# A hybrid decoder layer on one core: each head's first two token blocks projected side by side, and the norm's weights spread by TensorE

## The chip, the core and the metric

The kernel runs on one core of a Trainium2 chip. A core has five engines that run their own instruction streams in order: TensorE (PE in the profile, its weight loads PEld) multiplies matrices into PSUM, a memory of eight banks of 128 x 512 float32; VectorE (DVE), ScalarE (ACT) and GpSimd (POOL) work element by element; SyncE (SP) issues the DMA transfers here. They wait for each other by semaphores. The metric is the device time of one execution in microseconds.

## The reference

One layer of a decoder, in float32, over 1024 tokens of width 1024: an RMS norm, one wide input projection, two token mixers side by side, and a gated merge.

```python
h = rms_norm(x, norm_w)
proj = h @ w_in
q, k, v, z_a, xbc, z_s, dt_raw, gate_logits = split(proj)
# A: differential attention, 8 heads, two softmax maps per head
q, k = rms_norm(q, q_norm_w), rms_norm(k, k_norm_w)
a = softmax(q1 @ k1.T / 8) - lam * softmax(q2 @ k2.T / 8)      # causal
y_a = rms_norm(a @ v, subln_w) * 0.8 * silu(z_a)
# B: Mamba-2 scan, 32 heads in 4 groups, chunks of 128 tokens
x, B, C = split(silu(causal_conv(xbc)))
y_s = rms_norm((ssd_chunked(x, dt, A, B, C) + x * D) * silu(z_s), ssd_norm_w)
merged = sigmoid(g_a) * (y_a @ w_proj_attn) + sigmoid(g_s) * (y_s @ w_proj_ssd)
out = x + merged @ w_out
```

## The kernel before, in words

Every large product is made of three fast ones: each operand is split into a high part (rounded by ScalarE) and a low part (the rest, subtracted by VectorE or GpSimd), and TensorE adds high x high, high x low and low x high in one PSUM bank (`steps3`, L557; every matmul is recorded on L199, every transpose on L208).

A weight block is 128 rows by 512 columns. It is loaded raw from HBM (`w_loads`, four raw buffers for these), split into a slot (`w_splits`, L424; nine slots; every third block's low part is made on GpSimd, the others' on VectorE, L446), and its slot is given back by `w_done` (L546) when its last matmul has been issued. `w_need` (L540) waits for it.

The order of all instructions is written out by a planner (`Plan`, L79): generators for the bulk of TensorE's work and for all smaller tasks yield the time at which they can go on by the planner's own costs, and whichever is due emits its instructions next. On the chip each engine then keeps to that order. The bulk goes through these stages (`bulk`, L1757): the projections `pmz` of the first z groups and dt; twelve conv and gate pairs (`fX`, `fY`, `fZ`); eight heads (`att_proj`, L725) with attention and the scan worked in between as smaller tasks; then gates, output projections and the final product.

At the very start (`start`, L1778) SP issues the two halves of the first 128 tokens (x0), the norm's weights, four raw weight blocks and the other tokens. `prep_h` (L632) normalizes a block of 128 tokens: ScalarE squares and sums, GpSimd makes the root `rs`, VectorE multiplies x by `rs` and by the norm's weights (`stt`, L241, the tiles `nwb`), TensorE transposes the result (`ph`), and `h_evac` (L671) makes of it the high and low part, `hH` and `hL`, that all projections read. The norm's weights are 1024 numbers. Each half of them is loaded as 128 equal rows (L1781), 256 KB, and lies in SBUF until all eight blocks are prepared.

A head's projection (`att_proj`) takes for each of eight token blocks t the eight weight blocks kb in turn, three matmuls each, into one PSUM bank `pma`. In the first token block the weights are waited for, in the last one their slots are given back, one by one. After each token block `att_evac` (L748) is spawned: ScalarE squares q and k, takes z's tanh and copies v; VectorE sums the squares; GpSimd makes the root (`rs`, L265); VectorE scales q and k, after which the bank is free. PSUM banks are handed out by `trs`, eight in all, the bulk being served first. After four token blocks `qk_stack` transposes q and k and starts attention.

Of the kernel before, what the change touches and what calls it, by code (L numbers as in the profile page):

```python
# [139 lines left out]
def tile_hybrid_layer(ctx: ExitStack, tc: tile.TileContext, x, norm_w, w_in, q_norm_w, k_norm_w,  # L140
# [37 lines left out]
    def midt(shape=(P, 512), dt=F32, name="m"):  # L178
        return mid.tile(list(shape), dt, tag="b2", name=name)
# [31 lines left out]
    def pe_done():  # L211
        return pl.t + 0.2
# [40 lines left out]
    def load(o, i, after=0.0):  # L253
        nc.sync.dma_start(out=o, in_=i)
        q = pl.op("Q", 0.48, max(after, pl.t))
        n = o.free_size() * 512 / 360e3 if o.space != bass.MemoryType.DRAM else i.free_size() * 512 / 360e3
        return pl.op("D", n, q + 0.6) + lag[1]
# [282 lines left out]
    def w_need(i):  # L540
        while i not in w_at:
            yield pl.t + 0.1
        while w_at[i] > pl.t:
            yield w_at[i]
# [5 lines left out]
    def wide(i):  # L550
        return wts[i][:, 0].rearrange("p f c -> p (f c)"), wts[i][:, 1].rearrange("p f c -> p (f c)")
# [5 lines left out]
    def steps3(o, a, b, first, last, **kw):  # L557
        mm(o, a[0], b[0], first, False, **kw)
        yield
        mm(o, a[0], b[1], False, False, **kw)  # L560
        yield
        mm(o, a[1], b[0], False, last, **kw)
        yield
# [68 lines left out]
    def prep_h(t):  # L632
        while t not in xts:
            yield pl.t + 0.2
        xt, k, ats = xts[t]
        n = len(ats)
        parts = []
        for i, at in enumerate(ats):
            yield at
            ss = tin(1, "ss")  # L640
            xs = xt.rearrange("p (k c) -> p k c", k=KB)[:, i * KB // n:(i + 1) * KB // n]
            at = act(hL[:, i * KB // n:(i + 1) * KB // n, t * P:(t + 1) * P], xs, AF.Square, at,
                     scale=D ** -0.5, accum_out=ss)
            parts.append(ss)
        yield at
        rs = tin(1, "rs")
        if n > 1:
            at = stt(parts[0], parts[0], EPS, parts[1], ALU.add, ALU.add, at)
            yield at
            nc.gpsimd.tensor_tensor(out=rs, in0=parts[0], in1=mhalf[:, 0:1], op=ALU.pow)  # L650
            at = pl.op("G", 0.47, at)
        else:
            at = rsqrt(rs, parts[0], EPS, at)
        yield at
        pts = []
        nt = []
        for i in range(2):
            hs = slice(i * 512, i * 512 + 512)
            at = stt(xt[:, hs], xt[:, hs], rs, nwb[i], ALU.mult, ALU.mult, at - HOP if i else at)
            nt.append(at)  # L660
        for half in range(2):
            yield nt[half]
            kt = yield from pl.get(trs)
            pt = trt(f"ph{t}{half}")
            for i in range(4):
                tp(pt[:, i * P:(i + 1) * P], xt[:, (half * 4 + i) * P:(half * 4 + i + 1) * P])
            pts.append((pt, kt, pe_done()))
            pl.spawn(h_evac(t, half, *pts.pop()), pe_done())
        bigs.give(k, pl.t)
# [18 lines left out]
    def proj_tok(pm, t, ids, last):  # L688
        hb = lambda kb: (hH[:, kb, t * P:(t + 1) * P], hL[:, kb, t * P:(t + 1) * P])
        for kb in range(KB):  # L690
            yield from w_need(ids[kb])
            while (t, kb // 4) not in h_at:
                yield pl.t + 0.1
            while h_at[t, kb // 4] > pl.t:
                yield h_at[t, kb // 4]
            yield from steps3(pm, hb(kb), wide(ids[kb]), kb == 0, kb == KB - 1)
            if last:
                w_done(ids[kb])
# [26 lines left out]
    def att_proj(h):  # L725
        ids = w_next(KB)
        ks = []
        for _ in range(4):
            ks.append((yield from pl.get(heads)))
        v = bigt([P, NT, P], name=f"v{h}")  # L730
        zg = bigt([P, NT, P], name=f"zg{h}")
        kk = [bigt([P, S], F32R, name=f"kk{h}{m}") for m in range(2)]
        hd[h] = (v, zg, kk, ks)
        lefts[h] = [NT, {}]
        qk = []
        for t in range(NT):
            k = yield from pl.get(trs, first=True)
            pm = mmt(f"pma{h}{t}")
            yield from proj_tok(pm, t, ids, t == NT - 1)
            if t % 2 == 0:  # L740
                km = yield from pl.get(qkm)
                qk.append([midt([P, 2, 256], name=f"qk{h}{t}"), km, 0])
            pl.spawn(att_evac(h, t, pm, k, qk[-1][0][:, t % 2, :], qk[-1]), pe_done())
            if t % 4 == 3:
                pl.spawn(qk_stack(h, t // 4, qk), pl.t + 3.0)
                qk = []

    def att_evac(h, t, pm, k, qn, cell):  # L748
        v, zg = hd[h][0:2]
        at = pe_done()  # L750
        t2 = act(qn, pm[:, 0:256], AF.Square, at)
        t1 = act(zg[:, t, :], pm[:, 384:512], AF.Tanh, at, scale=0.5)
        tv = act(v[:, t, :], pm[:, 256:384], AF.Copy, at)
        yield t2
        ss = tin(4, "ss4")
        nc.vector.tensor_reduce(out=ss, in_=qn.rearrange("p (a d) -> p a d", a=4), axis=AX.X, op=ALU.add)
        t2 = pl.op("V", 0.335, t2)
        rs = tin(4, "rs4")
        yield max(t1, t2)
        t2 = rsqrt(rs, ss, 64 * EPS, t2)  # L760
        t1 = stt(zg[:, t, :], zg[:, t, :], 1.0, pm[:, 384:512], ALU.add, ALU.mult, t1)
        yield t2
        t2 = tt(qn.rearrange("p (a d) -> p a d", a=4), pm[:, 0:256].rearrange("p (a d) -> p a d", a=4),
                rs.unsqueeze(2).to_broadcast([P, 4, 64]), ALU.mult, t2)
        trs.give(k, max(t2, tv))
        cell.append(t2)

    def qk_stack(h, half, qk):
        v, zg, kk, _ = hd[h]
        lo, hi = slice(0, 64), slice(64, P)  # L770
        cs = slice(half * 512, half * 512 + 512)
        while len(qk[0]) < 5 or len(qk[1]) < 5 or "consts" not in ready:
            yield pl.t + 0.2
        yield max(qk[0][3:] + qk[1][3:] + [ready["consts"]])
        kq = yield from pl.get(bigs)
        kz = yield from pl.get(qlos)
        qh, ql = bigt([P, 2, 512], F32R, name=f"qh{h}{half}"), qlo[kz]
        done = []
        for isk in range(2):
            k = yield from pl.get(trs)  # L780
            pt = trt(f"pq{h}{half}{isk}")
            for i in range(4):
                tp(pt[:, i * P:(i + 1) * P], qk[i // 2][0][:, i % 2, isk * P:(isk + 1) * P])
            if isk:
                for c in qk:
                    qkm.give(c[1], pl.t + 0.1)
            at = pe_done()
            yield at
            t1 = at
            for m, (own, other) in enumerate(((lo, hi), (hi, lo))):  # L790
                if isk:
                    t1 = act(kk[m][own, cs], pt[own], AF.Copy, at)
                else:
                    act(qh[own, m], pt[own], AF.Copy, at, scale=wqk_c[own])
                    t1 = act(qh[other, m], pt[own], AF.Copy, at, scale=wqk_c[own])
            yield t1
            for m, (own, other) in enumerate(((lo, hi), (hi, lo))):
                if isk:
                    t1 = tt(kk[m][other, cs], pt[own], kk[m][own, cs], ALU.subtract, t1 - HOP)
                else:  # L800
                    t1 = stt(ql[own, m], pt[own], wqk_c[own], qh[own, m], ALU.mult, ALU.subtract, t1 - HOP)
            done.append(t1)
            trs.give(k, t1)
        pl.spawn(att_core(h, half, (qh, ql, kq, kz)), max(done))
# [967 lines left out]
            yield from products(c)  # L1772
        yield from final()

    kn = [mids.take() for _ in range(2)]
    nwb = [midt(name=f"nwb{i}") for i in range(2)]

    def start():  # L1778
        load_x(0)
        for i in range(2):  # L1780
            load(nwb[i], norm_w[:, i * 512:i * 512 + 512].partition_broadcast(P).rearrange("p a d -> p (a d)"))  # L1781
        yield from w_loads(0, 4)
        load_x(1)
        pl.spawn(prep_h(0))
        pl.spawn(prep_h(1), pl.t + 0.01)
        pl.spawn(w_splits(), pl.t + 0.02)
        yield from w_loads(4, 8)
        for t in range(2, NT):
            load_x(t)
            pl.spawn(prep_h(t))  # L1790
        while len(h_at) < 2 * NT:
            yield pl.t + 1.0
        for k in kn:
            mids.give(k, pl.t)

    def rest():
        yield pl.t + 8.0
# [34 lines left out]
```

## Time and profile before

| | us |
|---|---|
| median of 3 runs | 1624.73 (1622.62 to 1625.15) |
| the profiled execution | 1625.04 |
| its span, first to last instruction | 1623.3 |
| TensorE busy | 1589.2 (98%) |
| VectorE busy | 1088.5 (67%) |
| ScalarE busy | 915.1 (56%) |
| GpSimd busy | 706.9 (44%) |
| granted TensorE clock, mean | 0.996 of full |

A matmul's row lasts longer than its share of TensorE, since the next one starts before it ends: at full clock rows of 512 columns last about 0.39 us and start 0.23 us apart. Idle time in the views is time in which no row is open.

### The profile page before, as it was taken

To read this page: it belongs to the slowest core of one execution; us is meant where nothing else is said; L and a number is where in the kernel's file an instruction comes from. 1 tells how busy PE (TensorE), PEld (TensorE's weight loads), DVE (VectorE), ACT (ScalarE), POOL (GpSimd) and SP (SyncE) were. 2 spreads that over 40 slices of the span, in tenths; PEclk is the share of its full clock that TensorE was granted. 3 is DMA by queue.
4 is the path that set the end of the run, shared out by engine and by line. 5 is a ranking of instruction groups with operands and counts; after the bars stand their busy time and mean duration, and the time that the engine had idled before them with its cause. 6 is when DMAs were issued, how large, how long until landed. Compare 5 with 4: busy or idle time off the path is not lost.

```text
span 1623.3 us, 24344 instructions
## 1 busy us (share of the span) xinstructions
PE 1589.2 (98%) x8010; PEld 1330.2 (82%) x8010; DVE 1088.5 (67%) x2011; ACT 915.1 (56%) x2215; POOL 706.9 (44%) x847
## 2 busy tenths in 40 slices
PE   7999999999999999999989999999999999999999
PEld 5788888888788888887878888887887888888887
DVE  7836567537782576876767777876556577798831
ACT  7534447445563475786766777776666565352220
POOL 4315445334542543546475746464756433323000
PEclk9999999999999999999999999999999999999999
DMA  6213343533453461425163432433426397698941
GB/s 210 92 55 105 112 145 111 168 101 114 125 168 107 121 183 61 131 79 182 40 207 128 145 90 85 120 101 103 155 80 206 99 310 253 207 340 254 317 153 65
DMA packets 223804, 236.47 MB, mean 146 GB/s; under 512 B 15285, under 2 KB 155326, under 8 KB 223678
## 3 DMA queue, kind: packets, MB, share of 16 engines
q1 hardware_dynamic: 223678, 234.93, 45.6%
q8 instruction: 63, 1.03, 0.3%
q14 instruction: 63, 0.52, 0.1%
HBM read 164.48 MB, written 70.39 MB: 145 GB/s over the span
## 4 chain that ended last, share of the span: by engine, by line
PE 73%; DVE 3%; ACT 2%; POOL 2%; DMA 2%; issue 1%; SPq 0%; POOLq 0%; DVEq 0%; ACTq 0%
PE pma L199 18%; PE py L199 6%; PE pmz L199 5%; PE po L199 5%; PE pO L199 4%; PE pz L199 4%; PE px L199 4%; PE sc L199 4%; PE av L199 4%; PE fYc L199 3%; PE fXc L199 2%; PE pg L199 2%; PE pa L208 2%; PE fZc L199 2%; PE fYg L199 1%; PE pS L199 1%
## 5 line engine op out<-in xcount | busy, mean ns | idle before, releaser
L199 PE MATMUL pma<-w,hH 128*128 128x512 f32 x1024 | 345.2, 405 | 6.0 <-POOL w L233 5.4
L199 PEld LDWEIGHTS pma<-w,hH 128*128 128x128 f32 x1024 | 188.6, 189 | 40.9 <-POOL w L233 6.6
L199 PE MATMUL pma<-w,hL 128*128 128x512 f32 x512 | 206.8, 404 | 0.0
L199 PE MATMUL pmz<-w,hH 128*128 128x512 f32 x512 | 164.1, 398 | 0.7 <-ACT hH L225 0.7
L233 POOL TENSOR_TENSOR rawf<-rawf,rawf 128x512 f32<-128x512 f32 x54 | 71.6, 1326 | 166.4 <-DVE wp L233 87.8
L225 ACT ACTIVATE p<-p,nm 128x256 f32<-128x256 f32 (+7 forms) x128 | 98.6, 773 | 33.6 <-DVE nm L831 32.9
L225 ACT ACTIVATE w<-raw 128x512 fp32r<-128x512 f32 (+1 forms) x122 | 75.1, 626 | 75.0 <-DMA raw<-in_w_in_dram 28.7
L199 PEld LDWEIGHTS pmz<-w,hH 128*128 128x128 f32 x512 | 96.5, 190 | 20.6 <-ACT hH L225 1.1
L199 PEld LDWEIGHTS pma<-w,hL 128*128 128x128 f32 x512 | 96.8, 189 | 16.4
L233 POOL TENSOR_TENSOR w<-raw,w 128x512 fp32r<-128x512 f32 (+1 forms) x38 | 51.3, 1351 | 134.5 <-ACT w L225 120.7
L199 PE MATMUL fYc<-ft,wp 128*128 128x512 f32 x432 | 106.5, 392 | 0.7 <-DVE fu L233 0.7
L199 PE MATMUL pmz<-w,hL 128*128 128x512 f32 x256 | 101.4, 396 | 0.0
L199 PEld LDWEIGHTS fYc<-ft,wp 128*128 128x128 f32 x432 | 81.1, 189 | 17.9 <-DVE fu L233 1.1
L225 ACT ACTIVATE wp<-rawp 128x512 fp32r<-128x512 f32 x72 | 44.2, 626 | 84.1 <-POOL rawp L233 23.9
L233 DVE TENSOR_TENSOR wp<-rawf,wp 128x512 fp32r<-128x512 f32 x72 | 59.1, 837 | 34.7 <-ACT wp L225 34.7
L233 DVE TENSOR_TENSOR w<-raw,w 128x512 fp32r<-128x512 f32 (+1 forms) x84 | 65.1, 782 | 23.5 <-ACT w L225 23.3
L225 ACT ACTIVATE ab<-ab,nac 128x128 f32<-128x128 f32 x256 | 78.4, 392 | 1.7 <-POOL ab L1234 1.5
L199 PEld LDWEIGHTS av<-v,at 128*128 128x128 f32 x576 | 72.8, 191 | 6.5 <-ACT at L225 2.6
L265 POOL TENSOR_TENSOR rs<-rs,mhalf 128x4 f32<-128x4 f32 (+1 forms) x71 | 75.4, 1062 | 5.9
L225 ACT ACTIVATE wp<-rawf 128x512 fp32r<-128x512 f32 x108 | 65.9, 626 | 20.0 <-POOL rawf L233 16.4
L199 PE MATMUL av<-v,at 128*128 128x128 f32 x576 | 75.1, 275 | 1.7 <-ACT at L225 1.7
L831 DVE CUSTOM_DVE_ANT_0 p<-sc,maskb 128x512 f32<-128x512 f32 (+3 forms) x128 | 72.1, 584 | 6.2 <-PE sc L199 3.9
(299 smaller groups left out, 4217.8 us busy)
## 6 DMA issues: line engine op xcount, KB each, us to landing
raw<-in_w_in_dram SPq DMA_DIRECT2D x104, 256.0 KB, 3.6
rawf<-in_w_in_dram SPq DMA_DIRECT2D x72, 256.0 KB, 3.7
ab<-act_d SPq DMA_DIRECT2D x32, 512.0 KB, 4.9
cv_d<-cv SPq DMA_DIRECT2D x48, 256.0 KB, 2.1
t_d<-ts SPq DMA_DIRECT2D x24, 512.0 KB, 3.1
z_d<-zs SPq DMA_DIRECT2D x32, 256.0 KB, 2.0
xr<-cv_d SPq DMA_DIRECT2D x32, 256.0 KB, 3.0
zc<-z_d SPq DMA_DIRECT2D x32, 256.0 KB, 3.0
```

Source lines behind the costliest of these rows:

```text
L199: nc.tensor.matmul(o, lhsT=lhsT, rhs=rhs, start=start, stop=stop, **kw)
L208: nc.tensor.transpose(out=o, in_=i, identity=ident if idn is None else idn)
L225: nc.scalar.activation(o, i, f, **kw)
L233: (nc.vector if eng == "V" else nc.gpsimd).tensor_tensor(out=o, in0=a, in1=b, op=op)
L265: nc.gpsimd.tensor_tensor(out=dst, in0=dst, in1=mhalf[:, 0:cols], op=ALU.pow)
L831: nc.vector.tensor_tensor_reduce(out=p[:, j:e], in0=sc[i][:, 0:e - j], in1=maskb[:, S - n + j:S - n + e], scale=-1.0, scalar=nms[i - 1] if ...
```

## The change

Two things are changed. The heads' projections take the first two token blocks together: for each weight block kb first the three matmuls of block 0, then the three of block 1, into two PSUM banks. Blocks 2 to 7 go on as before. And the norm's weights are loaded as two rows of 512 numbers; a float32 matmul with a row of 128 ones spreads each to 128 rows of a PSUM bank, which VectorE then reads. The two banks are taken out of the eight until all token blocks are prepared. The two SBUF buffers that held the spread weights hold the rows now.

```diff
@@ prep_h
         pts = []
         nt = []
+        while "nwb" not in ready:
+            yield pl.t + 0.1
+        at = max(at, ready["nwb"])
+        yield at
         for i in range(2):
@@ att_proj
-        for t in range(NT):
-            k = yield from pl.get(trs, first=True)
-            pm = mmt(f"pma{h}{t}")
-            yield from proj_tok(pm, t, ids, t == NT - 1)
-            if t % 2 == 0:
-                km = yield from pl.get(qkm)
-                qk.append([midt([P, 2, 256], name=f"qk{h}{t}"), km, 0])
-            pl.spawn(att_evac(h, t, pm, k, qk[-1][0][:, t % 2, :], qk[-1]), pe_done())
-            if t % 4 == 3:
-                pl.spawn(qk_stack(h, t // 4, qk), pl.t + 3.0)
+        for ts in ((0, 1), (2,), (3,), (4,), (5,), (6,), (7,)):
+            pms = []
+            for t in ts:
+                k = yield from pl.get(trs, first=True)
+                pms.append((mmt(f"pma{h}{t}"), k))
+                if t % 2 == 0:
+                    km = yield from pl.get(qkm)
+                    qk.append([midt([P, 2, 256], name=f"qk{h}{t}"), km, 0])
+            for kb in range(KB):
+                yield from w_need(ids[kb])
+                for t, (pm, k) in zip(ts, pms):
+                    yield from steps3(pm, hblk(kb, t), wide(ids[kb]), kb == 0, kb == KB - 1)
+                    if kb == KB - 1:
+                        pl.spawn(att_evac(h, t, pm, k, qk[-1][0][:, t % 2, :], qk[-1]), pe_done())
+                if ts[0] == NT - 1:
+                    w_done(ids[kb])
+            if ts[-1] % 4 == 3:
+                pl.spawn(qk_stack(h, ts[0] // 4, qk), pl.t + 3.0)
                 qk = []
@@ before start
-    kn = [mids.take() for _ in range(2)]
-    nwb = [midt(name=f"nwb{i}") for i in range(2)]
+    kn, kb_ = [mids.take() for _ in range(2)], [trs.take() for _ in range(2)]
+    nwr = [midt([1, 512], name=f"nwr{i}") for i in range(2)]
+    nwb = [trt(f"nwb{i}") for i in range(2)]
+    one = const.tile([1, P], F32, name="one")
+    nc.gpsimd.memset(one, 1.0)
+
+    def norm_rows(t):
+        yield t
+        for i in range(2):
+            mm(nwb[i], one, nwr[i], True, True)
+        ready["nwb"] = pe_done()
@@ start
-            load(nwb[i], norm_w[:, i * 512:i * 512 + 512].partition_broadcast(P).rearrange("p a d -> p (a d)"))
+            t = load(nwr[i], norm_w[:, i * 512:i * 512 + 512])
+        pl.spawn(norm_rows(t), t)
```

Since the planner decides the order, its places move. On TensorE, the fourth head's first token block before: `pma30` and `pma31` are its first two token blocks, w76 to w83 its eight weight blocks, the other names attention and scan work of earlier heads.

```order
L199 MATMUL pma30_8248<-w76_7257,hH_111 128x512 x2
L199 MATMUL pma30_8248<-w76_7257,hL_112 128x512
L208 MATMUL pa230_8256<-ident_96,p23_8017 128x128 x4
L199 MATMUL pma30_8248<-w77_8141,hH_111 128x512 x2
L199 MATMUL pma30_8248<-w77_8141,hL_112 128x512
L199 MATMUL pma30_8248<-w78_8189,hH_111 128x512 x2
L199 MATMUL pma30_8248<-w78_8189,hL_112 128x512
L199 MATMUL av23_8275<-v2_7160,at230_8261 128x128 x4
```

Between the first matmul on w76 and the first on w78 stand six projection matmuls and one group of transposes. Now the same place on TensorE, from w77 on:

```order
L199 MATMUL pma30_8234<-w77_8096,hH_111 128x512
L199 MATMUL pma30_8234<-w77_8096,hL_112 128x512
L199 MATMUL pma31_8251<-w77_8096,hH_111 128x512 x2
L199 MATMUL pma31_8251<-w77_8096,hL_112 128x512
L199 MATMUL pma30_8234<-w78_8137,hH_111 128x512 x2
L199 MATMUL pma30_8234<-w78_8137,hL_112 128x512
L199 MATMUL pma31_8251<-w78_8137,hH_111 128x512 x2
L199 MATMUL pma31_8251<-w78_8137,hL_112 128x512
L199 MATMUL pma30_8234<-w79_8162,hH_111 128x512 x2
```

Each weight block is now followed by six matmuls instead of three before the next one is needed. On VectorE at the start before, the scalings of the last two token blocks (`x6`, `x7`) among the low parts `hL` of earlier ones, a block for dt (`w8`) and a small reduction:

```order
L233 TENSOR_TENSOR hL_112<-ph30_313,hH_111 128x4x128
L233 TENSOR_TENSOR hL_112<-ph31_321,hH_111 128x4x128
L241 SCALAR_TENSOR_TENSOR x6_200<-x6_200,rs_369,nwb0_118 128x512
L241 SCALAR_TENSOR_TENSOR x6_200<-x6_200,rs_369,nwb1_119 128x512
L233 TENSOR_TENSOR w8_349<-raw8_233,w8_349 128x4x32
L233 TENSOR_TENSOR hL_112<-ph40_353,hH_111 128x4x128
L233 TENSOR_TENSOR lp_273<-lamt_274 128x128
L312 TENSOR_REDUCE ls_408<-lp_273 128x2
L233 TENSOR_TENSOR hL_112<-ph41_362,hH_111 128x4x128
L241 SCALAR_TENSOR_TENSOR x7_202<-x7_202,rs_393,nwb0_118 128x512
```

and now the same place on VectorE:

```order
L233 TENSOR_TENSOR hL_112<-ph30_325,hH_111 128x4x128
L241 SCALAR_TENSOR_TENSOR x6_203<-x6_203,rs_374,nwb0_120 128x512
L241 SCALAR_TENSOR_TENSOR x6_203<-x6_203,rs_374,nwb1_121 128x512
L233 TENSOR_TENSOR hL_112<-ph31_334,hH_111 128x4x128
L233 TENSOR_TENSOR w8_357<-raw8_237,w8_357 128x4x32
L233 TENSOR_TENSOR hL_112<-ph40_361,hH_111 128x4x128
L241 SCALAR_TENSOR_TENSOR x7_205<-x7_205,rs_395,nwb0_120 128x512
```

The two pairs have moved ahead of one and of three other instructions, and the tiles `nwb0` and `nwb1` are PSUM banks. On ScalarE at the start, the splits `w0` to `w3` and the first copies `hH`, now (before, the split of `w2` stood behind the first copy):

```order
L225 ACTIVATE w0_151<-raw0_131 128x512
L225 ACTIVATE w1_156<-raw1_133 128x512
L225 ACTIVATE w2_164<-raw2_135 128x512
L225 ACTIVATE hH_111<-ph00_158 128x4x128
L225 ACTIVATE w3_173<-raw3_137 128x512
```

One split has moved ahead of the first copy. From the end of this start to the first head, and from the last head's end on, TensorE's order is that of before.

## Rows read from the trace of the kernel before

**Rows 1.** Busy time by stage (start, us, then each engine's busy time, clock, DMA).

```profile
0.00:40.00 40.00, 29.48 (x140) 22.61 (x141) 28.99 (x43) 30.72 (x58) 18.52 (x31) 1.00 0.65 213
40.00:598.00 558.00, 553.45 (x2548) 456.96 (x2547) 348.89 (x568) 287.06 (x549) 230.49 (x195) 0.99 0.39 119
598.00:1243.00 645.00, 631.37 (x3610) 538.94 (x3609) 453.04 (x1019) 448.44 (x1333) 357.86 (x542) 1.00 0.38 117
```

**Rows 2.** TensorE's waits, 598 to 1243 us (us, times, longest).

```profile
PE pma L199 <- POOL w L233: 5.4, 3, 2.3
PE pc L199 <- ACT yt L225: 2.3, 1, 2.3
...
PE pma L199 <- ACT w L225: 0.5, 1, 0.5
```

**Rows 3.** Timeline of TensorE, fourth head (start, us, what, count, idle before).

```profile
832.33 0.50 PE L199 MATMUL pma<-w,hH 128*128 128x512 f32 x1 [0.92 <-POOL w L233]
...
839.78 0.50 PE L199 MATMUL pma<-w,hH 128*128 128x512 f32 x1 [2.16 <-POOL w L233]
```

**Rows 4.** Busy time and granted clock of three stretches.

```profile
752.00:760.00 8.00, 5.70 (x30) 4.51 (x29) 3.58 (x5) 7.85 (x18) 5.74 (x5) 1.00 0.74 238
419.30:426.10 6.80, 6.80 (x24) 6.10 (x25) 4.31 (x9) 1.69 (x4) 0.00 (x0) 0.50 0.88 223
845.90:849.30 3.40, 3.02 (x9) 2.39 (x10) 3.23 (x5) 3.34 (x7) 2.49 (x3) 0.50 0.98 334
```

**Rows 5.** Timeline of TensorE, start.

```profile
7.56 2.33 PE L208 MATMUL ph<-ident,x 128*128 128x128 f32 x8 [7.56 <-DVE x L241]
10.64 1.22 PE L199 MATMUL pmz<-w,hH 128*128 128x512 f32 x2 [0.75 <-ACT hH L225]
...
15.50 0.63 PE L199 MATMUL pmz<-w,hL 128*128 128x512 f32 x1
...
17.54 0.40 PE L199 MATMUL pmz<-w,hL 128*128 128x512 f32 x1
17.77 0.40 PE L199 MATMUL pmz<-w,hH 128*128 128x512 f32 x1
```

**Rows 6.** Timeline of VectorE, start.

```profile
6.76 0.75 DVE L241 SCALAR_TENSOR_TENSOR x<-x,rs,nwb 128x512 f32<-128x512 f32 x1 [1.54 <-DMA nwb<-in_norm_w_dram]
7.97 0.75 DVE L241 SCALAR_TENSOR_TENSOR x<-x,rs,nwb 128x512 f32<-128x512 f32 x1 [0.46 <-DMA nwb<-in_norm_w_dram]
9.20 0.69 DVE L233 TENSOR_TENSOR w<-raw,w 128x512 fp32r<-128x512 f32 x1 [0.47 <-ACT w L225]
```

**Rows 7.** One tile's rows, `pacum`, float32 (ns min/median/max, first and last start).

```profile
L199 PE MATMUL pacum<-tv,tri x2: 377/378/378, 95.8 to 96.0; 128*128 128x256 f32 x2
```

**Rows 8.** DMA issues, 0 to 12 us (count, KB, us to landing), and SP's timeline.

```profile
x<-in_x_dram SPq DMA_DIRECT2D x2, 256.0 KB, 2.9
...
1.69 0.90 SPq L254 DMA_DIRECT2D nwb<-in_norm_w_dram  x2
```

**Rows 9.** GpSimd's rows on the tile `rs`, 598 to 1243 us.

```profile
L265 POOL TENSOR_TENSOR rs<-rs,mhalf x63: 1033/1045/1984, 604.7 to 1239.8; 128x4 f32<-128x4 f32 x63
```

**Rows 10.** VectorE's scalings, of the tiles `nwb` and `fXc`.

```profile
L241 DVE SCALAR_TENSOR_TENSOR x<-x,rs,nwb x16: 739/748/1783, 6.8 to 35.7; 128x512 f32<-128x512 f32 x16
...
L241 DVE SCALAR_TENSOR_TENSOR cv<-fXc,cols,cv x36: 733/742/751, 129.8 to 577.0; 128x511 f32<-128x511 f32 x12, 128x510 f32<-128x510 f32 x12, 128x509 f32<-128x509 f32 x12
```

**Rows 11.** Timelines of VectorE, GpSimd and TensorE, 29 to 38 us.

```profile
29.36 2.44 DVE L241 SCALAR_TENSOR_TENSOR x<-x,rs,nwb 128x512 f32<-128x512 f32 x2
...
34.74 2.76 DVE L241 SCALAR_TENSOR_TENSOR x<-x,rs,nwb 128x512 f32<-128x512 f32 x2
...
33.98 5.91 POOL L233 TENSOR_TENSOR r<-hH,hL 128x512 f32<-128x512 f32 x4 [1.03 <-DVE lp L233]
...
35.91 0.63 PE L208 MATMUL ph<-ident,x 128*128 128x128 f32 x4 [0.78 <-issue]
...
37.64 0.63 PE L208 MATMUL ph<-ident,x 128*128 128x128 f32 x4 [0.87 <-DVE x L241]
```

More of the change, by code (lines that the diff above doesn't have):

```diff
@@ L735, in att_proj, with hblk @@
         qk = []
-        for t in range(NT):
-            k = yield from pl.get(trs, first=True)
-            pm = mmt(f"pma{h}{t}")
-            yield from proj_tok(pm, t, ids, t == NT - 1)
-            if t % 2 == 0:
-                km = yield from pl.get(qkm)
-                qk.append([midt([P, 2, 256], name=f"qk{h}{t}"), km, 0])
-            pl.spawn(att_evac(h, t, pm, k, qk[-1][0][:, t % 2, :], qk[-1]), pe_done())
-            if t % 4 == 3:
-                pl.spawn(qk_stack(h, t // 4, qk), pl.t + 3.0)
+        for ts in ((0, 1), (2,), (3,), (4,), (5,), (6,), (7,)):
[16 more added lines that the diff above has]
+                pl.spawn(qk_stack(h, ts[0] // 4, qk), pl.t + 3.0)
                 qk = []
+    def hblk(kb, t):
+        return hH[:, kb, t * P:(t + 1) * P], hL[:, kb, t * P:(t + 1) * P]
     def att_evac(h, t, pm, k, qn, cell):
@@ L1792, in start @@
             yield pl.t + 1.0
-        for k in kn:
+        for k, b in zip(kn, kb_):
             mids.give(k, pl.t)
+            trs.give(b, pl.t)
     def rest():
```

## The prediction

> **What bounds the kernel now.** I read the busy time by stage first. The reader is to see that TensorE is the bound nearly everywhere: 553.5 of 558.0 us in the front-pair stage, 631.4 of 645.0 in the heads' stage, and 29.5 of 40.0 at the start [rows 1]; the last stage, 380 us behind the heads, looks like the second. So time can only come out of TensorE's idle time (34 us in all), and out of stretches in which its clock is at half. Two of the four stages are touched. The order of TensorE's instructions in the changed kernel is that of before from the end of the start to the first head, and again behind the last head, so I let those 558 and 380 us stand as they are, whatever they hold.
>
> Then I read who waited for whom in the heads' stage. Of its 13.6 us of idle time, 5.4 us are three waits of a head's matmul for a block of weights whose low part GpSimd makes, and 0.5 us one wait for a high part from ScalarE; the rest is spread over attention and state work, with one wait of 2.3 us for a scan chunk's product as its largest piece [rows 2]. The timeline of the fourth head's start shows two of them: the second matmul on block 2 (of 0 to 7) stands 0.92 us, that on block 5 2.16 us [rows 3]. All lie in a head's first token block. There eight blocks are taken in one pass, each for three matmuls, while their slots have only just come free in the last token block of the head before. From the second token block on all eight lie ready.
>
> [...]
>
> Last the start. TensorE's first row begins at 7.56 us, its first projection at 10.64 us, and its rows take 0.63 us each until 15.5 us and 0.40 from 17.5 us on: half clock first, full clock later [rows 5]. VectorE's first two scalings wait for the broadcast norm weights and end at 8.72 us, and the first subtraction of a weight block comes only at 9.20 us, since the weights queue behind those 512 KB [rows 6].
>
> **The change part by part.** First the heads. What it adds there is nothing: the same 1536 matmuls, in another order. The second token block's three matmuls on a block of weights are put behind the first's, so block n is first needed 3n matmuls later. Matmuls on these shapes start 0.23 us apart at full clock (17.54 and 17.77 [rows 5]), so three take 0.69 us. The wait on block 2 is moved by 1.4 us, against 0.92; that on block 5 by 3.4 us, against 2.16; the third, 2.3 us in the head before, is on block 7 and moved by 4.8 us. Each move exceeds its wait by half or more. What makes the blocks, the splits on ScalarE, VectorE and GpSimd, is paced by slots that come free in the head before, which is unchanged. So I take 5.4 us of the 5.9 as gone; the bounds are 5.9 (all) and 0 (the supply slips by as much).
>
> What is late next in this stage: both first blocks end three matmuls apart and are evacuated together. GpSimd's root takes 1.05 us for each [rows 9], and the second block's PSUM bank is held that much longer, while one bank more is held during the pass. With eight heads the bounds are 0 and 8 x 1.05 = 8.4 us if TensorE waited each time. Between them I take 0.7: in the trace other work of attention stands in a head's first blocks, and it fills such a gap as long as it has banks. For the rest of the stage, whose order is shuffled, I assume the old 7.7 us of other idle time; it could move by 3 us either way.
>
> The clock: 3.4 us at half cost 1.7 us [rows 4]. Two of the waits before it go, the scan product's 2.3 us may stay. I take half, 0.8 us, between 1.7 and 0; a new drop elsewhere, of 3.4 us or 6.8, would cost 1.7 to 3.4.
>
> Now the start. Removed: two transfers of 256 KB. Added: two of 2 KB, a memset, and two float32 matmuls of one row by 512 columns. A float32 product of 256 columns is two rows that start 0.2 us apart, so 0.4 us at full clock [rows 7]. At 512 columns that is 0.85, and at half clock 1.7 us each. A 256 KB transfer lands 2.9 us after its issue; by that the two rows, issued when the old ones were (two from 1.69 on, the second 0.45 later [rows 8]), are there by 4.6 and 5.05, the products at 6.3 and 8.0, and the two scalings end at 7.1 and 8.8, against 7.51 and 8.72. So the first transposes move hardly at all. If the small rows land 1 us later, so does all this; if earlier, up to 1 us is won. What does move is behind it: with the weights' raw blocks landing earlier, the first subtraction can follow the scalings at once, 8.8 instead of 9.20, and ScalarE, which now has three splits ahead of its first copy instead of two, finds them landed. Four weight blocks and x2 wait in SP's queue for these subtractions, so they are issued earlier by 0.4 and growing to about 1 us.
>
> VectorE's scalings are the other half. Alone one takes 0.74 to 0.75 us, but the slowest took 1.78 [rows 10]: the pairs at 29.36 and 34.74 took 2.44 and 2.76 us instead of 1.4 while GpSimd added hH and hL, and TensorE stood 0.78 and 0.87 us for transposes [rows 11]. 36 of the convolution's scalings, which read PSUM, never took over 0.751, with GpSimd at work in their stage too. So with the norm weights in PSUM I let the 2.4 us of excess go from VectorE (bounds 0 and 2.4).
>
> A scaling that reads PSUM took a median of 742 ns and one that reads SBUF alone 748 [rows 10], so I charge nothing for the other memory. [...]
>
> TensorE's idle time after its first projection is what these can give back: 10.5 us in the first 40 [rows 1], less 7.56 before its first row and 0.75 before the first projection, is 2.2, of which the two above are 1.65. I take 1.5, bounds 0 and 2.2. TensorE now begins 3 us earlier, so its clock may rise sooner; from 10.64 us to 16.5, the middle of the two rows that show half and full [rows 5], it lost half of 5.9, 2.9 us. I take a fifth, 0.6, bounds 0 and 2.9. The first projection itself waits for ScalarE's copy, which has the splits out of its way: 0.4, bounds -1 (small rows late) and 1. So the start gives 2.5 us, bounds -1 and 6.1. Two PSUM banks of eight are held until the last token block is prepared; the order of TensorE in the start shows the transposes no later than before relative to the projections, so I put nothing on it.
>
> **Sum**, against the profiled execution's own 1625.0 us (span 1623.3 and 1.7 around it): 5.4 + 0.8 + 2.5 - 0.7 = 8.0 us less, 1617.0. The median of the runs, 1624.7, lies 0.3 below that execution, which is inside the spread of the three.
>
> **Rivals.** (1) The waits come back in another place of the heads' stage: TensorE gets to the third token block as early as it saved, and stands there for attention's chains, whose speed the change does not touch. For it: 7.7 us of the stage's idle time are such waits. Against it: TensorE was busy 98% of the stage, so most chains are ahead of it. Then only the start pays: 1625.0 - 2.5 = 1622.5.
> (2) Slower: the double evacuation. The 8 PSUM banks run short behind each head's first pair, since the second block's bank waits for GpSimd's second root. It decides from the point where TensorE stands over 1 us per head, (5.4 + 2.5 + 0.8)/8 = 1.1. At 1.7 us per head, with other work of GpSimd's in between, it is 8 x 1.7 - 8.7 = 5 us slower: 1630. For it: GpSimd's roots already held VectorE in that stage. Against: the two roots together take 2.1 us, and the third token block's 24 matmuls that follow last at least 24 x 0.23 = 5.5.
> (3) The float32 products come late and the start gives nothing, while the heads pay: 1625.0 - 5.5 = 1619.5.
> (4) All pays: 5.9 of the waits, the drop's 1.7, and 4.5 at the start with an earlier full clock: 1613.
>
> **How the numbers follow.** Forecast 1617.0: chance 0.45, its own range 1614 to 1620. Rival 1: 0.20; rival 2: 0.13; rival 3: 0.10; rival 4: 0.12. A difference of 0.2% (3.2 us) is about what can be told from none here. Faster by more than that: forecast, rivals 3 and 4, and a quarter of rival 1, 0.72. Within: the rest of rival 1, 0.15. Slower: 0.13. The range leaves out the outer half of rival 4 and most of rival 2: 1610 to 1626.
>
> **What would show it.** Right: no wait of a head's matmul for w on GpSimd over 0.5 us in the heads' stage; TensorE idle there 8 to 9 us instead of 13.6; no 0.50 stretch near 846 us, the one near 419 still there, some 2 us earlier; scalings all at 0.75 us; no stand of TensorE at 34 to 38 us; the first head's first matmul 2 to 3 us before 597.8. Wrong: new waits for pma or its evacuation behind each head's first pair; or waits for sc, pa, av that have grown by as much as w lost; the first transposes later than 8.5 us.

## The result and the profile after

The changed kernel took 1614.34 us (median of 4 runs, 1612.54 to 1615.75), the kernel before 1623.67 beside it (4 runs, 1620.62 to 1625.15). The ratio is 0.9944 with a 95% interval of 0.9926 to 0.9963: faster by 0.56%, 9 us. Timed again later, the changed kernel took 1614.28 us and the ratio was 0.9946 (0.9933 to 0.9958). Forecast were 1617.0 us and a range of 1610 to 1626.

Of the changed kernel, busy time by stage, cut at its own first and last matmul of the heads (`pma`): start and end in us, length, busy time of PE, PEld, DVE, ACT, POOL with instructions, granted clock, DMA share, GB/s. The last row is the heads' stage of before, cut in the same way.

```profile
0.00:40.00 40.00, 34.65 (x158) 25.41 (x159) 27.68 (x50) 33.03 (x60) 15.78 (x32) 1.00 0.60 200
40.00:591.70 551.70, 547.17 (x2534) 451.35 (x2533) 346.22 (x561) 284.81 (x546) 232.75 (x195) 1.00 0.40 120
591.70:1227.70 636.00, 626.07 (x3597) 535.05 (x3596) 454.20 (x1016) 445.52 (x1330) 356.05 (x539) 1.00 0.38 118
```

```profile
597.80:1239.30 641.50, 627.87 (x3595) 536.35 (x3594) 452.21 (x1015) 447.22 (x1329) 354.50 (x536) 1.00 0.38 116
```

TensorE's idle time in the heads' stage fell from 641.50 - 627.87 = 13.6 us to 9.9, and the stage from 641.5 to 636.0. What it waits for there now, of the changed kernel (us in total, times, longest):

```profile
PE py L208 <- ACT xn L225: 2.8, 3, 1.3
PE av L199 <- ACT at L225: 1.5, 1, 1.5
PE pb L208 <- ACT yt L225: 1.3, 1, 1.3
PE pya L208 <- ACT at L225: 1.2, 1, 1.2
PE pa L208 <- DVE p L241: 1.0, 2, 0.6
```

The waits of `pma` for w, first in [rows 2], are gone without a rest. So is the wait of `pc`, second there with 2.3 us. In their place stand waits of attention and of the scan for ScalarE. They are of two kinds. `py` and `av` wait for an operand (`xn`, `at`) that ScalarE makes. `pb` and `pya`, as `pc` before, read nothing that the named instructions write: as the program has it, they wait for a bank of PSUM that ScalarE copies out (`yt` out of an earlier `pya`, `at` out of an earlier `pa`). One wait for an operand falls into the fourth head's first pair, where [rows 3] had the waits for blocks 2 and 5 (timeline of TensorE; the bracket is the idle time before and what ended it):

```profile
823.63 0.40 PE L199 MATMUL pma<-w,hH 128*128 128x512 f32 x1
825.37 0.66 PE L208 MATMUL py<-ident,xn 128*128 128x128 f32 x4 [1.34 <-ACT xn L225]
```

The clock near [rows 4], of the changed kernel: neither stretch is at half in this execution. In a second profiled execution of the same kernel the one behind 416 us is there again. First the changed kernel's first profiled execution, then its second:

```profile
419.30:426.10 6.80, 6.80 (x33) 5.60 (x33) 4.83 (x9) 3.13 (x7) 4.95 (x5) 1.00 0.54 172
845.90:849.30 3.40, 3.40 (x18) 2.83 (x18) 3.02 (x13) 1.37 (x5) 3.23 (x4) 1.00 0.39 154
```

```profile
416.00:424.00 8.00, 7.95 (x29) 6.98 (x30) 4.43 (x10) 2.88 (x6) 0.48 (x2) 0.57 0.80 256
845.90:849.30 3.40, 3.40 (x19) 2.87 (x17) 3.34 (x9) 1.75 (x7) 3.16 (x4) 1.00 0.61 241
594.60:1230.50 635.90, 626.06 (x3597) 535.08 (x3597) 454.77 (x1016) 445.54 (x1330) 355.65 (x539) 1.00 0.38 118
```

The start of the changed kernel, TensorE, for [rows 5]:

```profile
4.06 3.75 PE L199 MATMUL nwb<-nwr,one 1*128 1x512 f32 x4 [4.06 <-DMA nwr<-in_norm_w_dram]
7.74 2.03 PE L208 MATMUL ph<-ident,x 128*128 128x128 f32 x8
9.54 1.22 PE L199 MATMUL pmz<-w,hH 128*128 128x512 f32 x2
...
12.48 0.40 PE L199 MATMUL pmz<-w,hL 128*128 128x512 f32 x1
...
31.24 0.66 PE L208 MATMUL ph<-ident,x 128*128 128x128 f32 x4 [0.17 <-DVE hL L233]
```

The first transposes come 0.18 us later than before, the first projection 1.1 us earlier, and rows of 0.40 us from 12.5 instead of about 17 us. (For the first 40 us both profiles print a granted clock of 1.00; that the start ran at half is read from the rows alone: those of 512 columns last 0.63 us and start 0.43 apart, as they do before in the stretch at 419.3 that is printed at 0.50, against 0.40 and 0.23.) VectorE's scalings, for [rows 10], and what GpSimd did beside the last of them, for [rows 11]:

```profile
L241 DVE SCALAR_TENSOR_TENSOR x<-x,rs,nwb x16: 734/740/748, 6.2 to 31.8; 128x512 f32<-128x512 f32 x16
...
28.75 5.08 POOL L233 TENSOR_TENSOR r<-hH,hL 128x512 f32<-128x512 f32 x4
...
31.10 1.40 DVE L241 SCALAR_TENSOR_TENSOR x<-x,rs,nwb 128x512 f32<-128x512 f32 x2
```

No scaling is stretched, and none of the stands of 0.78 and 0.87 us is left. The first conv pair's first matmul (`fXc`) shows what the start gave, ahead of any difference in the clock of the middle stage; first before, then after (ns min/median/max, first and last start in us):

```profile
L199 PE MATMUL fXc<-hH,wp x192: 387/389/774, 120.5 to 563.8; 128*128 128x512 f32 x192
```

```profile
L199 PE MATMUL fXc<-hH,wp x192: 387/389/481, 117.3 to 557.5; 128*128 128x512 f32 x192
```

So the start is 3.2 us shorter in this pair of executions. Single executions differ: `fXc` begins at 120.5, 121.5 and 121.8 us in three with the old start, and between 117.3 and 118.3 us in nine with the new one. The first head begins 6.1 us earlier (591.7), but 2.9 of these are the half clock of [rows 4] that this execution did not have; in the second execution, which had it, it begins at 594.6, 3.2 us earlier.

### The profile page after: what moved, and what is told of

Read it like the earlier page. It is cut to its first block, busy times and chain, and to the rows that moved or that the text cites. A ratio compares the mean times of both kernels' runs of the same rounds, so it can differ in the third digit from the quotient of the medians.

```text
span 1610.8 us, 24386 instructions
## 1 busy us (share of the span) xinstructions
PE 1585.9 (98%) x8014; PEld 1326.2 (82%) x8014; DVE 1090.0 (68%) x2011; ACT 913.1 (57%) x2215; POOL 709.0 (44%) x848
## 4 chain that ended last, share of the span: by engine, by line
PE 70%; ACT 4%; POOL 4%; DVE 3%; issue 1%; DMA 0%; SPq 0%; DVEq 0%; ACTq 0%; POOLq 0%
PE pma L199 16%; PE py L199 6%; PE pmz L199 5%; PE po L199 5%; PE pz L199 4%; PE px L199 4%; PE pO L199 4%; PE sc L199 4%; PE av L199 3%; PE fYc L199 3%; PE pg L199 2%; PE fXc L199 2%; PE fZc L199 2%; PE pa L208 1%; PE fYg L199 1%
## 5 line engine op out<-in xcount | busy, mean ns | idle before, releaser
L225 ACT ACTIVATE p<-p,nm 128x640 f32<-128x640 f32 (+7 forms) x128 | 98.7, 774 | 39.5 <-DVE nm L846 39.0
L233 DVE TENSOR_TENSOR w<-raw,w 128x512 fp32r<-128x512 f32 (+1 forms) x84 | 69.2, 841 | 16.8 <-ACT w L225 16.7
L233 POOL TENSOR_TENSOR rawp<-rawp,rawp 128x512 f32<-128x512 f32 x36 | 55.0, 1543 | 53.4 <-DVE wp L233 46.6
```

The costliest lines, as they stand in the source:

```text
L225: nc.scalar.activation(o, i, f, **kw)
L233: (nc.vector if eng == "V" else nc.gpsimd).tensor_tensor(out=o, in0=a, in1=b, op=op)
```

## Experiments

Ratios are to the kernel before, timed beside each, with 95% intervals. They are estimates of their own, and the quotient of the two medians can lie 0.1% off.

**One part alone.** The first kernel is the kernel before with the heads' part, the second that with the norm's part:

```diff
 e1: att_proj
+        for ts in ((0, 1), (2,), (3,), (4,), (5,), (6,), (7,)):
...
 e2: start
+            t = load(nwr[i], norm_w[:, i * 512:i * 512 + 512])
+        pl.spawn(norm_rows(t), t)
```

> The kernel before with the heads' part of the change alone; the start and all up to the first head keep the order of before. Theory (the weight waits go because each block is needed later): 5 to 6 us faster than before, about 1618; in the heads' stage no wait for w over 0.5 us (5.9 before in all), other waits 8 to 10 us, and no half-clock stretch near 846 us. Rival (the heads' gain in the changed kernel came from the start's shift or from a lucky new order): within 2 us of before, waits for w still 3 us or more, or other waits up by 5.

> The kernel before with the norm's part alone; from the end of the start on, heads included, TensorE keeps the order of before. Theory (the start gains by lighter transfers, by scalings that GpSimd does not stretch, and by an earlier full clock, and a TensorE-bound kernel carries all of it to the end): 3.2 us faster, about 1620.5; scalings all under 0.76 us, full clock by 13 us, the waits for w in the heads as before, 5 to 6 us. Rival (the later stages absorb it): within 1 us of before.

Heads alone: 1616.44 us against 1623.83, 0.9964 (0.9950 to 0.9978). Norm alone: 1618.78, 0.9967 (0.9955 to 0.9978). 0.36% and 0.33% add up to 0.69%, against 0.56% measured for both; the intervals allow it. TensorE's waits in the heads' stage with the norm's part alone, and with the heads' part alone:

```profile
PE pma L199 <- POOL w L233: 5.2, 3, 2.3
PE av L199 <- ACT at L225: 1.7, 3, 1.0
```

```profile
PE py L208 <- ACT xn L225: 2.8, 3, 1.3
PE av L199 <- ACT at L225: 1.5, 1, 1.5
PE pb L208 <- ACT yt L225: 1.3, 1, 1.3
```

The three waits for w go with the heads' part alone, and the same new ones come with it. `fXc` begins at 121.8 us with the heads' part, at 117.5 with the norm's: each part acts in its own stage. (The first of these executions has a stretch of 3.4 us at half clock from 37.4 us on, with a mean granted clock of 0.97 in its first 40 us, which the others have not.) The norm's part alone came out 1.7 us below the 1620.5 that were expected; no run here says why.

**More pairs.** Is it the double evacuation that costs (rival 2)?

```diff
-        for ts in ((0, 1), (2,), (3,), (4,), (5,), (6,), (7,)):
+        for ts in ((0, 1), (2, 3), (4, 5), (6,), (7,)):
```

> The changed kernel with token blocks 2, 3 and 4, 5 side by side too. No wait for weights is at stake there, but each head has three double evacuations instead of one. Theory (a double evacuation costs TensorE next to nothing): 1614, give or take 3 for the new order. Rival (the second bank, held for GpSimd's second root, makes TensorE stand 1 us each time): 16 more of them, about 1630.

1617.34 us, 0.9963 (0.9949 to 0.9977), about 3 us above the changed kernel and 6 below the one before. Two more pairs in each head are far from the 5 us over before that rival 2 gave for one. Idle time in the heads' stage is 635.00 - 626.64 = 8.4 us, less than the 9.9 with one pair. The second view shows a wait that one pair had not:

```profile
592.90:1227.90 635.00, 626.64 (x3581) 532.34 (x3580) 450.18 (x1014) 442.20 (x1323) 347.85 (x534) 1.00 0.38 118
```

```profile
PE pma L199 <- ACT at L225: 2.6, 3, 1.3
```

These are waits for a bank, and they stand right behind a pair, at the first matmul of block 6 (1.3 us), 4 (1.0) and 5 (0.3). So a shortage of banks behind pairs exists, at 2.6 us for 24 pairs; but what is awaited is ScalarE's copy for attention, not GpSimd's second root. The 3 us above the changed kernel don't show in the heads' stage of the profiled execution: its last stage took 386.3 us (1614.2 - 1227.9), against 383.1.

**The wait taken away at its other end.** The kernel before, but VectorE makes all low parts from the heads' blocks on. (The edit also takes the later blocks from GpSimd; before, it made six of them behind 1245 us.)

```diff
-            t = tt(lo, raw, hi, ALU.subtract, t, "G" if i >= NW and i % WPOOL == 0 else "V")
+            t = tt(lo, raw, hi, ALU.subtract, t, "G" if NW <= i < NFRONT - 64 and i % WPOOL == 0 else "V")
```

> The kernel before, with the low parts of all heads' weight blocks made on VectorE; every third was on GpSimd. Theory A (the blocks are late because a low part stands in GpSimd's queue behind scan work that waits itself): the waits for w fall to under 1.5 us in all, VectorE is busy 16 us more in the stage, the time 1618 to 1623. Theory B (the blocks are late because their slots come free too late, whichever engine splits): waits for w stay at 4 us or more, now put down to VectorE, and the time is 1624 or above.

1613.44 us (6 runs, 1611.18 to 1619.35), 0.9946 (0.9929 to 0.9963), without the norm's part. TensorE's waits in the heads' stage:

```profile
PE pO L199 <- DVE ab L233: 2.4, 1, 2.4
PE pma L199 <- DVE w L233: 1.1, 1, 1.1
PE pma L199 <- ACT w L225: 0.6, 1, 0.6
```

The waits for w fall from 5.9 to 1.7 us (theory A: under 1.5). So most of them were GpSimd's, and taking the low parts from it pays at least what the pair pays. That the median lies some 5 us below theory A's range is not explained.

**Where the norm's weights lie.** The changed kernel, with ScalarE copying the two PSUM banks to SBUF, where the scalings read them:

```diff
+            nc.scalar.activation(nws[i], nwb[i], AF.Copy)
```

> The changed kernel, but ScalarE copies each of the two PSUM banks into an SBUF tile and the scalings read that. Two 2 KB transfers as in the changed kernel, norm weights in SBUF as before. Theory P (the stretched scalings came from VectorE and GpSimd working on SBUF together): the pairs that stand beside GpSimd rows take 2.4 to 2.8 us again, the mean of the 16 rises from 0.74 to about 0.89 us, and TensorE stands at about 30 to 35 us again for one or two transposes; the first projection is later by the copies, 0.6 to 1 us. Ratio to before 0.9955 to 0.997 against 0.9944 of the changed kernel. Theory L (only the lighter transfers counted, the stretch was contention with the DMA's 512 KB): the scalings stay at 0.75 us, no stand at 30 to 35, ratio 0.9945 to 0.9955.

1614.49 us, 0.9945 (0.9927 to 0.9962): as the changed kernel. Its scalings, and one pair of them:

```profile
L663 DVE SCALAR_TENSOR_TENSOR x<-x,rs,nws x16: 739/746/1174, 6.9 to 34.1; 128x512 f32<-128x512 f32 x16
...
33.03 1.84 DVE L663 SCALAR_TENSOR_TENSOR x<-x,rs,nws 128x512 f32<-128x512 f32 x2
```

The stretch comes back, in one pair of eight, which GpSimd's additions (31.08 to 33.66 and from 34.35 us on) overlap for 1.2 us. In the changed kernel a pair lay wholly beside such additions and took 1.40. That supports theory P for the stretch itself, by one pair on each side. But most of it had gone without PSUM: the other pairs lie ahead of GpSimd's additions in this order. No stand of TensorE at 30 to 35 us came of it. The first projection, at 10.54 us, and `fXc`, at 118.3, begin 1.0 us later than in the changed kernel, behind the copies. Theory L is nearer in time.

**An earlier clock.** Five extra matmuls on TensorE ahead of the norm's rows:

```diff
+        for _ in range(5):
+            nc.tensor.matmul(nwb[0], lhsT=maskb[:, 0:P], rhs=maskb[:, 0:512], start=True, stop=True)
```

> The changed kernel with five extra bf16 matmuls on TensorE before the two rows of the norm's weights arrive; their result is written over. Theory C (TensorE's earlier first row brought the full clock earlier, 12.4 to 15.1 us in the runs that had it, 13.5 to 16.5 in those that had not): full clock now from 8 to 12 us, the rows of the first projections 0.40 us instead of 0.63, and the first head's first matmul 0.5 to 1.5 us earlier than the 591.7 us of the changed kernel, with no half clock between; ratio to before 0.993 to 0.9945. Rival D (the clock's rise at the start goes by something else than TensorE's early rows): full clock at 12 to 15 us as before, no gain, ratio 0.9944.

1613.37 us, 0.9941 (0.9926 to 0.9956), no difference from the changed kernel. TensorE, start of this kernel:

```profile
2.01 2.31 PE L1804 MATMUL nwb<-maskb 128*128 128x512 bf16 x5 [2.01 <-POOL maskb L276]
...
12.08 0.40 PE L199 MATMUL pmz<-w,hL 128*128 128x512 f32 x1
```

Rows of 0.40 us begin at 12.08 instead of 12.48 us, and `fXc` at 117.8 instead of 117.3. Theory C isn't borne out: work ahead of the norm's rows did not make the start shorter.

**Both remedies, one, and the pair elsewhere.** Three kernels with the norm's part and all low parts from the heads' blocks on made on VectorE: with the first two token blocks side by side, with none, and with blocks 2 and 3.

```diff
 first pair:  for ts in ((0, 1), (2,), (3,), (4,), (5,), (6,), (7,)):
 no pair:     for t in range(NT):
 later pair:  for ts in ((0,), (1,), (2, 3), (4,), (5,), (6,), (7,)):
```

> The changed kernel with all low parts of the heads' weight blocks on VectorE instead of every third on GpSimd. Theory A (what the heads' part removes is the wait for GpSimd's low parts, 5 to 6 us, and moving them to VectorE removes the same wait, plus 3 us of what else waited for GpSimd): the two do not add up; norm's part 5.4 + 8.8 measured for VectorE's low parts alone = 14 us less than before, 1609.5, ratio 0.9913 (0.990 to 0.993). Rival B (they act on different waits): 5.4 + 5.9 + 8.8 = 20 us less, 1603.7, ratio 0.9876. Rival V (six matmuls per block and more work on VectorE delay the evacuations): no better than the changed kernel, 0.9944 or above.

> The kernel before with the norm's part and with all low parts of the heads' weight blocks on VectorE; its heads take the token blocks one by one. Theory A: the same as the one with the first two blocks side by side, 1609.5, ratio 0.9913 (0.990 to 0.993), and short waits of pma for w on VectorE of 1 to 2 us in all that the side by side order would not have. Rival B: 5.9 us slower than that one, ratio about 0.9913 against 0.9876.

First pair: 1616.11 us, 0.9956 (0.9942 to 0.9971). No pair: 1611.55, 0.9923 (0.9907 to 0.9940). The two remedies don't add up: together they are 4.6 us worse than the second alone. Theory A and rival B both expected less for the first pair; the nearest was rival V, though no evacuation of a head's block is waited for in its trace: its largest wait in the heads' stage is `pa <- ACT at`, 2.5 us, for a bank that ScalarE's copy gives back, followed by 3.4 us at half clock from 884.7 on. But the heads' stage is not where the two profiled executions part: it took 633.9 us with the first pair and 633.2 without. The first-pair kernel has another wait behind the last head, with half clock right behind it (1246.5 to 1249.9 us), and the one without a pair has neither:

```profile
1246.45 0.42 PE L199 MATMUL sc<-kk,qh 128*128 128x128 f32 x1 [3.27 <-DVE kk L233]
```

So attention work that the heads leave over can also cost time in the last stage, which the prediction let stand.

The 4.6 us raised the question whether a pair costs by itself.

> The norm's part, all low parts of the heads' blocks on VectorE, and the third and fourth token blocks (2 and 3) side by side instead of the first two. No weight block is waited for there, so this pair can gain nothing; it shows what two banks filled and evacuated together cost. Theory E (a pair costs 3 to 5 us wherever it stands, by the 4.6 us between the kernel with the first pair and the one without, and the 3 us that two more pairs cost): 1614.5 to 1616.5, ratio 0.994 to 0.9955. Rival F (only a pair at a head's start costs, where the blocks' slots come free): 1611.5, ratio 0.9923.

> The changed kernel itself, timed beside the other two on one chip: 1614.3, ratio 0.9944.

> The norm's part and all low parts of the heads' blocks on VectorE, token blocks one by one, timed beside the changed kernel on one chip: 1611.5, ratio 0.9923, 2 to 4 us below the changed kernel, if the removed wait and not the side by side order is what pays in the heads' stage; equal to it within 1 us otherwise. If a half-clock stretch of 10 us near 836 shows again, as in both earlier executions with these low parts, it follows from a stand of 2.7 us for the scan product and costs about 4 us.

Later pair: 1607.80 us, 0.9904 (0.9888 to 0.9919). Changed kernel: 1614.28, 0.9946. No pair: 1612.21, 0.9934 (0.9921 to 0.9946). Theory E falls, and rival F with it: the later pair gains 4.4 us. TensorE in the heads' stage and in one stretch of it, without and with the later pair:

```profile
595.00:1228.20 633.20, 624.73 (x3572) 536.83 (x3571) 458.14 (x1035) 446.06 (x1320) 326.46 (x516) 0.99 0.38 119
836.70:846.90 10.20, 7.68 (x31) 7.11 (x31) 8.24 (x12) 6.11 (x11) 1.74 (x3) 0.50 0.89 273
```

```profile
594.70:1224.10 629.40, 624.08 (x3573) 532.30 (x3572) 461.75 (x1035) 442.72 (x1320) 326.91 (x515) 1.00 0.38 119
836.70:846.90 10.20, 10.11 (x57) 8.24 (x56) 9.90 (x21) 6.65 (x15) 9.63 (x11) 1.00 1.05 351
```

Without a pair TensorE stands several times between 826 and 840 us (1.52, 0.57, 1.09, 0.47 and 2.52 us), and the clock is at half for 10.2 us; with the later pair these stands do not meet, and TensorE idles 5.3 us in the stage instead of 8.5. The stage is 3.8 us shorter, of the 4.4 in the medians. So what this pair gains is, as far as these traces show, the order that it gives the stands, at that one place.

**The pair moved in the changed kernel.** The last kernel asks whether the changed kernel's gain is that of any other order:

```diff
-        for ts in ((0, 1), (2,), (3,), (4,), (5,), (6,), (7,)):
+        for ts in ((0,), (1,), (2, 3), (4,), (5,), (6,), (7,)):
```

> The changed kernel with the pair moved: token blocks 2 and 3 side by side, the first two one by one again; every third low part on GpSimd as in the changed kernel. Theory W (the changed kernel gains in the heads' stage because a block is needed only after six matmuls): the waits of pma for w on GpSimd are back, 4 to 6 us in some three waits, and the time is that of the norm's part alone, 1618 to 1619.5, ratio 0.9965 to 0.9975. Theory O (any other order of the stage does as well, by where its stands happen to fall): waits for w of under 2 us, or other waits smaller by as much, 1614 or below, ratio 0.9945 or below.

1623.68 us, 0.9994 (0.9982 to 1.0005), 9 us above the changed kernel. TensorE's waits in the heads' stage, the fourth head's first block, and the two stretches at half clock:

```profile
PE av L199 <- ACT at L225: 4.2, 1, 4.2
PE pma L199 <- DVE w L233: 2.7, 2, 2.0
PE pma L199 <- POOL w L233: 2.2, 2, 1.4
```

```profile
828.82 0.50 PE L199 MATMUL pma<-w,hH 128*128 128x512 f32 x1 [1.41 <-POOL w L233]
...
832.78 0.50 PE L199 MATMUL pma<-w,hH 128*128 128x512 f32 x1 [0.77 <-POOL w L233]
...
835.95 0.50 PE L199 MATMUL pma<-w,hH 128*128 128x512 f32 x1 [0.70 <-DVE w L233]
838.95 0.50 PE L199 MATMUL pma<-w,hH 128*128 128x512 f32 x1 [2.03 <-DVE w L233]
```

```profile
839.50:842.90 3.40, 3.40 (x14) 2.92 (x13) 2.05 (x3) 2.71 (x4) 0.00 (x0) 0.50 1.08 318
1098.90:1105.80 6.90, 4.22 (x14) 3.54 (x15) 4.65 (x8) 4.82 (x16) 4.61 (x6) 0.51 0.57 162
```

Theory W holds in its main sign: with the first block alone the waits for w are back, 4.9 us of them, and the half clock right behind. Only 2.2 of them are for GpSimd, though; 2.7 are for low parts that VectorE made. Theory O falls: this other order does not do as well. But W's time was 4 to 6 us too low: one new wait of 4.2 us for attention, with 6.9 us at half clock around it, came with this order. This stands against the norm's part alone (1618.8), which has the waits for w but not that one.

## Why the prediction was right

The steps, as the profiled executions show them (us; minus is less time):

| term | predicted | measured |
|---|---|---|
| heads' waits for w | -5.4 | -5.9 |
| half clock near 846 | -0.8 | -1.7 |
| start | -2.5 | -3.2 |
| other waits of the heads' stage | +0.7 | +2.2 |
| sum | -8.0 | -8.6 |
| half clock behind 416, in a stage not touched | 0 | -2.9 |
| last stage | 0 | -0.9 |

The spans of the two executions differ by 1623.3 - 1610.8 = 12.5 us, which the table gives within 0.1; the medians differ by 9.3, nearest to the sum of the terms that the change has touched. The other two are the luck of one execution: the second profiled execution of the changed kernel had the half clock behind 416 again. That the sum came so near is luck in part, too: the gains were 2.1 us larger than forecast and the counter-term 1.5 us, and the two misses nearly cancel.

Waits for w: right, by the mechanism named. They are gone with a pair at the head's start, and there in the kernels that have none and keep GpSimd's low parts (5.2 us with the norm's part alone, 4.9 with the pair moved). All 5.9 went, which fits that each move exceeded its wait.

The clock: right in kind, half in size. The 1.7 us of the table are an estimate, half of the 3.4 us at 0.50 [rows 4]; TensorE's busy time in the heads' stage fell by 627.87 - 626.07 = 1.8 us. The stretch near 846 did not come in either profiled execution, nor in that of the heads' part alone. The half was taken since the scan product's wait of 2.3 us (`pc`), at whose end the stretch begins, might stay; it went, too. Which of the waits brought the drop is not shown. With the norm's part alone, which keeps the waits for w and has none of `pc`, the clock is at half just behind two of them, that on block 7 in the third head and that on block 5 in the fourth:

```profile
752.40:755.80 3.40, 3.40 (x11) 2.82 (x10) 1.63 (x3) 3.34 (x9) 2.18 (x2) 0.50 0.57 201
837.70:841.10 3.40, 3.40 (x12) 2.63 (x11) 0.42 (x1) 1.06 (x3) 1.18 (x2) 0.50 1.00 326
```

In the kernel before, the first of these waits, of the same 2.3 us, had no half clock behind it: 1.00 from 752 to 760 us [rows 4].

The double evacuation was the wrong name for the counter-term. No wait right behind a first pair is one for a bank; those in or near the first blocks are `av` and `py`, for operands of attention and the scan. The two waits for a bank, `pb` 1.3 and `pya` 1.2, stand at 874 and 984 us, in the fifth and in the seventh block of their heads. The 2.2 us are a balance: `pc`'s 2.3 went, and 4.5 net of other waits came. That is rival 1's mechanism, at a third of its size (2.2 of 5.9). It is why TensorE idles 9.9 us there, above the 8 to 9 that were named. The term was too small.

The start: its sum was 0.7 us too small, and its parts were sized wrongly. The first projection came 1.1 us earlier instead of 0.4. The idle time behind it fell by 0.9, from 2.2 to 1.3, instead of 1.5: the two large stands went, but five waits of 0.16 to 0.48 us came. The full-speed rows some 4 us earlier leave about 1.2 of the 3.2, instead of 0.6. That TensorE's earlier first row brought them is not shown: with five matmuls ahead its first row began 2.05 us earlier still (2.01 against 4.06 us), while its rows of 0.40 us came 0.40 us sooner (12.08 against 12.48). That nothing was charged for scalings that read PSUM is borne out: their median was 740 ns with the norm's weights in PSUM and 746 with them in SBUF, in nearly equal starts.

Named as signs and seen: no wait for w, no half clock near 846, scalings of 0.74 us throughout, no stands at 34 to 38. Not as named: the first head 6.1 instead of 2 to 3 us earlier, of which 3.2 is the start's; no half clock near 419 in this execution; and 9.9 us of idle time in the heads' stage.

What stays open is how much of one order's time is chance. The place of one pair changed the median by -9.4 us (first instead of later, GpSimd's low parts), by +4.6 (first instead of none, VectorE's) and by -4.4 (later instead of none, VectorE's). The removed waits for w explain some 5 of the first; the rest are single stands of 2 to 4 us, with half clock behind, that fall in some orders and not in others, and for the +4.6 most of what the traces show lies behind the heads. No run here foretells where.

## What to carry to other kernels

A wait for an operand that comes in order is best moved by placing independent work between its uses, and the check is simple: each move, in instructions times their spacing, against the wait that it covers. Take away a named wait first, then read where the others have gone, since here two remedies for one wait did not add up. And where a planner reorders a whole stage, put a margin of some 5 us on each new order, and time a few of them: here the best was the norm's part, VectorE's low parts and the later pair together, at 0.9904.

## What the runs showed of the hardware beyond that

The same stand ahead of the same instructions was followed by full clock in one profiled execution of the changed kernel and by half clock in the other. TensorE in the first, and in the second:

```profile
416.11 1.97 PE L199 MATMUL pO<-xdt,ab 128*128 128x64 f32 x16 [2.50 <-DVE cv L241]
```

```profile
416.05 3.38 PE L199 MATMUL pO<-xdt,ab 128*128 128x64 f32 x16 [2.50 <-DVE cv L241]
```

The stand is 2.50 us in both, and the sixteen rows behind it take 1.97 or 3.38 us. Of the first heads' starts, 591.7 and 594.6, this makes the whole difference, 2.9 us: more than most terms of the sum. Of the fourteen profiled executions of this case, which all have this stand, of 2.50 or 2.51 us, eight have 6.8 us at half clock behind it, four have 3.4, and two, that of the changed kernel above and that of the heads' part alone, have none.

A float32 matmul of one row by 512 columns is two rows in the trace, as one of 256 columns was; the four took 3.75 us, near the 2 x 1.7 us that the prediction put down at half clock, and the two small rows of weights landed by 4.06 us.

GpSimd's additions were faster, too, in the start where VectorE reads the norm's weights from PSUM: four of them took 5.08 us beside the pair of scalings of 1.40, against 5.91 beside the pair of 2.76 [rows 11]. Other rows of VectorE lie beside both, so that the scalings are the cause is not shown.
